# Attention stage: all value products of a unit in one step, the transposes one step later, their split two steps later

## The chip, the cores and the metric

The kernel runs on one core of a Trainium2 chip. The metric is device time in microseconds, the median of three runs. One further execution was recorded by the hardware profiler; its rows are what this text reads.

## What is computed

Two residual layers over 2,048 latent and 256 context tokens of width 1,024. The first is a state-space mixer, the second is grouped-query attention. The change touches the second layer's softmax attention alone:

```
grp = 16 // 4                        # 16 query heads, 4 key/value heads, head size 64
def block(qi):                       # 128 queries
    s = einsum('bqkgd,bskd->bkgqs', qi, k).astype(f32) * 64 ** -0.5    # against 2304 keys
    p = softmax(s, axis=-1)
    return einsum('bkgqs,bskd->bqkgd', p, v)
```

The output of attention is gated, multiplied by the output weights, added to the residual and normalized.

## The kernel before

All of attention is `odd_attention` (from line 1905). A **unit** is one query head with 128 queries against all 2,304 keys, so there are 16 query tiles x 16 heads = 256 units. A unit goes through these steps, each a small function:

- `s_step(u, b)`, for b = 0, 1, 2: four float32 matmuls on TensorE (PE) give the scores of 768 keys in PSUM tile `s` (two buffers). A VectorE (DVE) instruction copies them to `st` (`st0`, `st1`, `st2`, two buffers each) and folds the running maximum into `mx` (L2002). After b = 2 a small DVE instruction makes the exponent's bias of it (L2006).
- `exp_step(u, b)`: ScalarE (ACT) takes the exponential in place (L2010). It needs the bias of L2006.
- `n_step(u, b)` and `d_step(u, b)`, b = 0, 1: GpSimd (POOL) splits the first six (b = 0) or four (b = 1) chunks of 128 keys into a high and a low float16 part (L2017, L2018), and a transposing DMA on SP's queue turns them into `T` (L2022).
- `t_step(u)`: PE transposes the other eight chunks into PSUM tile `tp` (one buffer, L2029).
- `split_step(u)`: ACT copies `tp` to float16 `hi` (L2034). `lower_step(u)`: DVE subtracts, `lo = tp - hi` (L2039). `hi` and `lo` have two buffers.
- `pv_step(u, g)`: products with the values, accumulated in PSUM tile `pv` (one buffer), two for each chunk, one with the high part (129 columns, L2058) and one with the low part (65 columns, L2060). Group g = 0 uses the six chunks of the first DMA (12 products), g = 1 the four of the second (8 products), g = 2 the eight of `hi` and `lo` (16 products). In group 2 the first product takes `hi` and the second takes `lo`.
- `pv_end(u)`: ACT copies the result out (L2073); every fourth unit adds a DVE reciprocal and three small POOL instructions.

The order on every engine is the program order, written by hand: a loop makes one **round** of three steps for each u. In round u the scores are those of unit u + 2, the exponentials those of unit u + 1, the transposes those of unit u, the value products those of unit u - 1. The functions are called in the order shown in the diff below; each call appends to the queues of its engines.

At the end of a step, entries of `todo` follow. `finish` spreads the output projection of a query tile (16 units) over the next rounds: transposes of the result `pt` at step 2 of two rounds, then 16 times three matmuls into `po` (L2116 to L2118), 14 of them at step 2 of consecutive rounds and two at step 1 of two of these rounds, then the normalization, of which `end` (ACT L2127, DVE L2128) stands at step 1 of two rounds. In the first 17 rounds `out_weights` also splits the output weights, at the start of step 2 (ACT L1449, DVE L35 `wl`).

Of the kernel before, what the change touches and what calls it, by code (L numbers as in the profile page):

```python
# [1904 lines left out]
def odd_attention(E, out):  # L1905
    nc, I, S, tc = E.nc, E.I, E.S, E.tc
    v, gp = nc.vector, nc.gpsimd
    with ExitStack() as ctx:
# [38 lines left out]
        def values(i):  # L1947

            cs = slice(3 * i, 3 * i + 3)
            x = RAWV[:, cs].rearrange("p c (k d) -> p (c k) d", d=HD)  # L1950
            vv = V2[:, cs].rearrange("p c k e -> p (c k) e")
            nc.scalar.activation(out=vv[:, :, 0:64], in_=x, func=AF.Copy, scale=E.vscale[:, 0:1])
            if i in VPOOL:
                gp.tensor_scalar(out=x, in0=x, scalar1=E.vscale[:, 0:1], scalar2=0.0, op0=ALU.mult, op1=ALU.add)
                gp.tensor_tensor(out=vv[:, :, 65:129], in0=x, in1=vv[:, :, 0:64], op=ALU.subtract)
            else:
                v.scalar_tensor_tensor(out=vv[:, :, 65:129], in0=x, scalar=E.vscale[:, 0:1], in1=vv[:, :, 0:64],
                                       op0=ALU.mult, op1=ALU.subtract)
# [3 lines left out]
        def out_weights(u, b):  # L1962

            n = u - 1
            k, half = divmod(n, 2)
            if b == 0 and half == 1 and 0 <= k + 1 < KC:
                OW[k + 1] = sp.tile([P, DM], F32, tag=("oh", "ol")[k % 2], name="wr", bufs=1)
                nc.sync.dma_start(out=OW[k + 1], in_=I["od_wo"][:, k + 1])
            if b == 0 and n == 0:
                for w in ("wh", "wl"):  # L1970
                    W[w] = (wp if w == "wh" else vp).tile([P, KC, DM], F32R, tag=w, name=w)
            if b == 2 and 0 < n <= 2 * KC:
                kk, h = divmod(n - 1, 2)
                cs = slice(h * 512, h * 512 + 512)
                split_raw(nc, v, W["wh"][:, kk, cs], W["wl"][:, kk, cs], OW[kk][:, cs])
            if b == 2 and 0 <= n < 2 * KC:
                cs = slice(half * 512, half * 512 + 512)
                gp.tensor_tensor(out=OW[k][:, cs], in0=OW[k][:, cs], in1=gate[:, cs], op=ALU.mult)
# [5 lines left out]
        def unit(u):  # L1984
            return u // 16, (u // 4) % 4, u % 4

        def s_step(u, b):

            qt, kv, hh = unit(u)
            if b == 0:  # L1990
                if hh == 0 and u // 4 + 1 < 64:
                    load_q(u // 4 + 1)
                UN[u] = dict(mx=kp.tile([P, 8], F32, tag="mx", name="mx", bufs=4), st=[None] * NTH)
            U, Q = UN[u], QB[u // 4]
            st = U["st"][b] = pp.tile([P, TH], F32, tag=f"st{b}", name="st", bufs=2)
            mx = U["mx"]
            ps = sps.tile([P, 1024], F32, tag="s", name="s", bufs=2)
            for c0, n in ((0, 512), (512, TH - 512)):
                for i in range(2):
                    nc.tensor.matmul(ps[:, c0:c0 + n], Q[:, hh % 2, i, hh // 2], KS[kv][:, b * TH + c0:b * TH + c0 + n],  # L2000
                                     start=(i == 0), stop=(i == 1))
            v.tensor_tensor_reduce(out=st, in0=ps[:, :TH], in1=zero.to_broadcast([P, TH]), scale=1.0,  # L2002
                                   scalar=NEG if b == 0 else mx[:, b - 1:b], op0=ALU.add, op1=ALU.max,
                                   accum_out=mx[:, b:b + 1])
            if b == NTH - 1:
                v.tensor_scalar(out=mx[:, 6:7], in0=mx[:, b:b + 1], scalar1=-1.0, scalar2=LOGP, op0=ALU.mult, op1=ALU.add)  # L2006

        def exp_step(u, b):
            st = UN[u]["st"][b]
            nc.scalar.activation(out=st, in_=st, func=AF.Exp, bias=UN[u]["mx"][:, 6:7])  # L2010

        def n_step(u, b):

            n = DCH[b] * P
            nat = UN[u]["nat", b] = pp.tile([P, 2, n], F16, tag=f"nat{b}", name="nat", bufs=2)
            p = UN[u]["st"][b][:, :n]
            gp.tensor_scalar(out=nat[:, 0], in0=p, scalar1=1.0, scalar2=0.0, op0=ALU.mult, op1=ALU.add)  # L2017
            gp.tensor_tensor(out=nat[:, 1], in0=p, in1=nat[:, 0], op=ALU.subtract)  # L2018
# [12 lines left out]
        def split_step(u):  # L2031
            hi, lo = [pp.tile([P, TCH, P], F16, tag=n, name=n, bufs=2) for n in ("hi", "lo")]
            pt = UN[u]["pt"]
            nc.scalar.activation(out=hi, in_=pt, func=AF.Copy)  # L2034
            UN[u]["hl"] = hi, lo
# [5 lines left out]
        def pv_step(u, g):  # L2041

            qt, kv, hh = unit(u)
            if g == 0:
                UN[u]["pv"] = sps.tile([P, 130], F32, tag="pv", name="pv", bufs=1)
            pv = UN[u]["pv"]
            c0, n = ((0, DCH[0]), (DCH[0], DCH[1]), (DCH[0] + DCH[1], TCH))[g]
            for k in range(n):
                c = c0 + k
                if g < 2:  # L2050
                    hi, lo = [UN[u]["T", g][:, i * n + k, :] for i in range(2)]
                else:
                    hi, lo = [t[:, k] for t in UN[u]["hl"]]
                first = g == 0 and k == 0
                end = g == 2 and k == n - 1
                for w in (0, 1) if first else (1, 0) if k == n - 1 else (0, 1):
                    if w == 0:
                        nc.tensor.matmul(pv[:, 0:129], hi, V2[:, c, kv, 0:129], start=first, stop=end)  # L2058
                    else:
                        nc.tensor.matmul(pv[:, 0:65], lo, V2[:, c, kv, 0:65], start=False, stop=False)  # L2060

        def pv_end(u):
            qt, kv, hh = unit(u)
            pv = UN[u]["pv"]
            if u % 16 == 3:
                QT[qt] = sp.tile([P, DM], F32, tag="o", name="o", bufs=1)
            if u % 16 == 0:
                SG[qt] = sp.tile([P, DM], F32, tag="sg", name="sg", bufs=1)
                nc.sync.dma_start(out=SG[qt], in_=S["sg"][qt * P:(qt + 1) * P, :])
            if hh == 0:  # L2070
                QR[kv % 2] = sp.tile([P, 4, 130], F32, tag="r", name="r")
            R = QR[kv % 2]
            nc.scalar.activation(out=R[:, hh, 0:129], in_=pv[:, 0:129], func=AF.Copy)  # L2073
            if hh == 3:
                oc = QT[qt][:, kv * 256:(kv + 1) * 256].rearrange("p (h d) -> p h d", d=HD)
                rs = sp.tile([P, 4, 1], F32, tag="rs", name="rs")
                v.reciprocal(rs, R[:, :, 64:65])
                of = QT[qt][:, kv * 256:(kv + 1) * 256]
                sgk = SG[qt][:, kv * 256:(kv + 1) * 256]
                small.extend([  # L2080
                    lambda: gp.tensor_tensor(out=oc, in0=R[:, :, 0:64], in1=R[:, :, 65:129], op=ALU.add),
                    lambda: gp.tensor_tensor(out=oc, in0=oc, in1=rs.to_broadcast([P, 4, HD]), op=ALU.mult),
                    lambda: gp.tensor_tensor(out=of, in0=of, in1=sgk, op=ALU.mult)])
            del UN[u]
            if u % 16 == 15:
                finish(qt, u + 1)
# [64 lines left out]
        for i in range(-2 * NTH, (NU + 2) * NTH):  # L2151
            u, b = divmod(i, NTH)
            if 0 <= i + VSTEP < NS // 3:
                values(i + VSTEP)
            out_weights(u, b)
            live = lambda w: 0 <= w < NU
            if live(u + 2):
                s_step(u + 2, b)
            if b == 1 and live(u):
                split_step(u)  # L2160
            if b == 2 and live(u - 1):
                pv_end(u - 1)
            if live(u + 1):
                exp_step(u + 1, b)
                if b < NTH - 1:
                    n_step(u + 1, b)
            if b == 0 and live(u):
                t_step(u)
            if live(u - 1):
                for g in ((0,), (1, 2), ())[b]:  # L2170
                    pv_step(u - 1, g)
            if live(u + 1) and b < NTH - 1:
                d_step(u + 1, b)
            if b == 1 and live(u):
                lower_step(u)
            if small:
                small.pop(0)()
            for f in todo.pop((u, b), []):
                f()
# [16 lines left out]
def tile_hybrid(ctx, tc, I, out, phases=None, preload=None, dumps=None):  # L2196
# [60 lines left out]
    if on("F"):  # L2257
        odd_attention(E, out)
# [78 lines left out]
```

## Time and profile before

| | |
|---|---|
| time, median of 3 runs | 3898.3 us (3897.76 to 3899.44) |
| the profiled execution | 3896.1 us, span of its instructions 3894.3 us |
| mean granted TensorE clock | 0.983 |
| PE matmul busy | 3692.1 us, 95% of the span |
| DVE busy | 2684.5 us, 69% |
| ACT busy | 1860.5 us, 48% |
| POOL busy | 2192.1 us, 56% |
| attention | about 2430 us to the end |

Busy time is what an engine spends in instructions; the span is from the first to the last instruction. Overlapping matmuls make PE's busy time say little of its reserve: start-to-start times of consecutive groups say more. A DVE or ACT instruction may start a little before the end of the one ahead of it on the same engine.

### The profile page before, as it was taken

To read this page: it belongs to the slowest core of one execution; us is meant where nothing else is said; L and a number is where in the kernel's file an instruction comes from. 1 tells how busy PE (TensorE), PEld (TensorE's weight loads), DVE (VectorE), ACT (ScalarE), POOL (GpSimd) and SP (SyncE) were. 2 spreads that over 40 slices of the span, in tenths; PEclk is the share of its full clock that TensorE was granted. 3 is DMA by queue.
4 is the path that set the end of the run, shared out by engine and by line. 5 is a ranking of instruction groups with operands and counts; after the bars stand their busy time and mean duration, and the time that the engine had idled before them with its cause. 6 is when DMAs were issued, how large, how long until landed. Compare 5 with 4: busy or idle time off the path is not lost. (4 is left out here: it accounts for less than half of the span.)

```text
span 3894.3 us, 72153 instructions
## 1 busy us (share of the span) xinstructions
PE 3692.1 (95%) x27102; PEld 3133.9 (80%) x27102; DVE 2684.5 (69%) x5008; ACT 1860.5 (48%) x3227; POOL 2192.1 (56%) x2120
## 2 busy tenths in 40 slices
PE   7999999977888999999999999799999999999998
PEld 4888886536887888788778887689999999999997
DVE  5367666887786888611354544778888888888885
ACT  4422223424335656311232222667777777777775
POOL 2111113662334999422333323888888888888886
PEclk9999999999999999999999999999999999999999
DMA  7522323335666776534332223998899999999996
GB/s 264 181 61 60 95 78 108 112 116 137 215 228 237 240 240 232 197 115 135 121 119 87 82 91 119 201 153 163 159 169 159 168 166 161 165 158 163 161 166 120
DMA packets 998589, 594.48 MB, mean 153 GB/s; under 512 B 711848, under 2 KB 908248, under 8 KB 996192
## 3 DMA queue, kind: packets, MB, share of 16 engines
q1 hardware_dynamic: 984112, 563.35, 59.7%
q10 hardware_dynamic: 14128, 26.51, 1.9%
q8 instruction: 214, 3.51, 0.4%
q14 instruction: 135, 1.11, 0.1%
HBM read 296.63 MB, written 125.32 MB: 108 GB/s over the span
## 5 line engine op out<-in xcount | busy, mean ns | idle before, releaser
L2010 ACT ACTIVATE st<-st,mx 128x768 f32<-128x768 f32 x768 | 714.3, 930 | 350.2 <-DVE mx L2006 246.0
L2018 POOL TENSOR_TENSOR nat<-st,nat 128x768 f16<-128x768 f32 (+1 forms) x512 | 732.7, 1431 | 42.7
L2000 PE MATMUL s<-KS,q 128*128 128x512 f32 (+1 forms) x3072 | 707.4, 353 | 17.0 <-DVE mx L2002 16.7
L2002 DVE CUSTOM_DVE_ANT_0 st<-s,zero,mx 128x768 f32<-128x768 f32 x512 | 518.9, 1013 | 241.3 <-POOL nat L2017 98.7
L2000 PEld LDWEIGHTS s<-KS,q 128*128 128x128 f32 x3072 | 538.6, 189 | 112.9 <-DVE mx L2002 23.3
L2017 POOL TENSOR_SCALAR nat<-st 128x768 f16<-128x768 f32 (+1 forms) x512 | 378.7, 740 | 128.0 <-ACT st L2010 125.4
L2058 PE MATMUL pv<-V,T 128*128 128x129 f16 x2560 | 310.1, 222 | 14.1 <-DMA T<-nat 14.1
L2039 DVE TENSOR_TENSOR lo<-tp,hi 128x1024 f16<-128x1024 f32 x256 | 312.3, 1220 | 4.6 <-ACT hi L2034 4.6
L41 PE MATMUL mmps<-ah,wh 128*128 128x512 f32 (+1 forms) x800 | 304.6, 381 | 3.8 <-DVE ah L214 3.8
L42 PE MATMUL mmps<-al,wh 128*128 128x512 f32 (+1 forms) x800 | 298.9, 374 | 0.1
L43 PE MATMUL mmps<-ah,wl 128*128 128x512 f32 (+1 forms) x800 | 298.7, 373 | 0.0
L2029 PE MATMUL tp<-ident,st 128*128 128x128 f32 x2048 | 274.7, 275 | 9.9 <-ACT st L2010 5.6
L41 PE MATMUL mm<-w,ah 128*128 128x512 f32 x656 | 263.5, 402 | 1.6 <-ACT ah L1679 1.6
L42 PE MATMUL mm<-w,ah 128*128 128x512 f32 x656 | 256.7, 391 | 2.3 <-DVE w L35 2.3
L2034 ACT ACTIVATE hi<-tp 128x1024 f16<-128x1024 f32 x256 | 257.4, 1006 | 2.7 <-PE tp L2029 1.0
L43 PE MATMUL mm<-w,al 128*128 128x512 f32 x656 | 257.1, 392 | 0.0
L2058 PEld LDWEIGHTS <-T 128*128 128x128 f16 x2560 | 233.6, 97 | 27.2 <-DMA T<-nat 16.2
L2002 DVE CUSTOM_DVE_ANT_0 st<-s,zero 128x768 f32<-128x768 f32 x256 | 243.6, 952 | 13.2 <-PE s L2000 7.3
L2060 PE MATMUL pv<-V,T 128*128 128x65 f16 x2560 | 249.1, 193 | 0.0
L277 DVE SCALAR_TENSOR_TENSOR acc<-raw,convw,acc 128x512 f32<-128x512 f32 (+1 forms) x320 | 223.4, 698 | 35.8 <-POOL raw L270 11.9
L2029 PEld LDWEIGHTS tp<-ident,st 128*128 128x128 f32 x2048 | 229.0, 141 | 22.7 <-ACT st L2010 12.8
L2058 PE MATMUL pv<-V,hi 128*128 128x129 f16 x2048 | 220.3, 220 | 0.0
(431 smaller groups left out, 9006.5 us busy)
## 6 DMA issues: line engine op xcount, KB each, us to landing
ac<-acs SPq DMA_DIRECT2D x72, 512.0 KB
q<-q SPq DMA_DIRECT2D x128, 256.0 KB
x<-xn SPq DMA_DIRECT2D x35, 512.0 KB
h<-h SPq DMA_DIRECT2D x34, 512.0 KB
x<-in_x_dram SPq DMA_DIRECT2D x32, 512.0 KB
adaw<-in_ada_w_dram SPq DMA_DIRECT2D x32, 512.0 KB
a<-aT SPq DMA_DIRECT2D x32, 512.0 KB
wr<-in_ev_w_dram SPq DMA_DIRECT2D x38, 256.0 KB
```

Of the source, the lines that this page charges most:

```text
L41: nc.tensor.matmul(ps, ah(k), bh(k), start=first and k == 0, stop=False)
L42: nc.tensor.matmul(ps, ah(k), bl(k), start=False, stop=False)
L43: nc.tensor.matmul(ps, al(k), bh(k), start=False, stop=last and k == n - 1)
L2000: nc.tensor.matmul(ps[:, c0:c0 + n], Q[:, hh % 2, i, hh // 2], KS[kv][:, b * TH + c0:b * TH + c0 + n], start=(i == 0), stop=(i == 1))
L2002: v.tensor_tensor_reduce(out=st, in0=ps[:, :TH], in1=zero.to_broadcast([P, TH]), scale=1.0, scalar=NEG if b == 0 else mx[:, b - 1:b], op0= ...
L2010: nc.scalar.activation(out=st, in_=st, func=AF.Exp, bias=UN[u]["mx"][:, 6:7])
L2017: gp.tensor_scalar(out=nat[:, 0], in0=p, scalar1=1.0, scalar2=0.0, op0=ALU.mult, op1=ALU.add)
L2018: gp.tensor_tensor(out=nat[:, 1], in0=p, in1=nat[:, 0], op=ALU.subtract)
L2029: nc.tensor.transpose(pt[:, j], UN[u]["st"][b][:, k * P:(k + 1) * P], E.ident)
L2034: nc.scalar.activation(out=hi, in_=pt, func=AF.Copy)
L2039: v.tensor_tensor(out=lo, in0=UN[u]["pt"], in1=hi, op=ALU.subtract)
L2058: nc.tensor.matmul(pv[:, 0:129], hi, V2[:, c, kv, 0:129], start=first, stop=end)
```

## The change

Only the order of the calls within a round, the order of the three product groups, and with it the product that closes the accumulation:

```
-                end = g == 2 and k == n - 1
+                end = g == 1 and k == n - 1
...
             if live(u + 2):
                 s_step(u + 2, b)
-            if b == 1 and live(u):
+            if b == 2 and live(u):
                 split_step(u)
-            if b == 2 and live(u - 1):
+            if b == 1 and live(u - 1):
                 pv_end(u - 1)
             if live(u + 1):
                 exp_step(u + 1, b)
                 if b < NTH - 1:
                     n_step(u + 1, b)
-            if b == 0 and live(u):
+            if b == 0 and live(u - 1):
+                for g in (0, 2, 1):
+                    pv_step(u - 1, g)
+            if b == 1 and live(u):
                 t_step(u)
-            if live(u - 1):
-                for g in ((0,), (1, 2), ())[b]:
-                    pv_step(u - 1, g)
             if live(u + 1) and b < NTH - 1:
                 d_step(u + 1, b)
-            if b == 1 and live(u):
+            if b == 2 and live(u):
                 lower_step(u)
```

Of the engines' queues in a round, with the step's number behind each entry:

```
       before                                             after
PE     s0, T, g0 | s1, g1, g2 | s2                        s0, g0, g2, g1 | s1, T | s2
ACT    exp0 | split, exp1 | pv_end, exp2                  exp0 | pv_end, exp1 | split, exp2
DVE    r0 | r1, lower | r2, bias                          r0 | r1 | r2, bias, lower
```

Here r0 to r2 are the DVE copies of the three score tiles (L2002), and the bias is L2006.

## Rows read from the trace of the kernel before

**Rows 1.** Windows: length, busy PE, PEld, DVE, ACT, POOL, clock, DMA share.
```profile
2470.00:2500.00 30.00, 25.74 (x261) 22.36 (x259) 24.31 (x41) 17.95 (x26) 26.48 (x25) 0.91 1.15 221
2500.00:2530.00 30.00, 25.74 (x278) 21.73 (x278) 25.04 (x47) 20.62 (x30) 29.25 (x28) 1.00 0.78 156
...
2636.40:3778.00 1141.60, 1135.90 (x12381) 1033.81 (x12380) 937.24 (x1795) 823.68 (x1118) 997.31 (x1015) 1.00 0.92 163
```

**Rows 2.** Waits, 2647.7 to 3789: engine, line, releaser, total, times, longest.
```profile
PE s L2000 <- DVE mx L2002: 5.7, 13, 0.5
```

**Rows 3.** Timeline of PE, first transposes of units 0, 32 and 112.
```profile
2434.98 1.91 PE L2029 MATMUL tp<-ident,st 128*128 128x128 f32 x8
...
2636.47 1.04 PE L2029 MATMUL tp<-ident,st 128*128 128x128 f32 x8
...
3075.52 1.04 PE L2029 MATMUL tp<-ident,st 128*128 128x128 f32 x8
```

**Rows 4.** Timeline of PE, one round: start, length, instruction.
```profile
3048.07 1.04 PE L2029 MATMUL tp<-ident,st 128*128 128x128 f32 x8
3048.94 0.22 PE L2058 MATMUL pv<-V,T 128*128 128x129 f16 x1
...
3049.43 0.95 PE L2000 MATMUL s<-KS,q 128*128 128x512 f32 x4
3050.22 0.23 PE L2058 MATMUL pv<-V,T 128*128 128x129 f16 x1
...
3050.64 0.19 PE L2060 MATMUL pv<-V,lo 128*128 128x65 f16 x1
...
3051.25 0.94 PE L2000 MATMUL s<-KS,q 128*128 128x512 f32 x4
...
3052.72 0.86 PE L2000 MATMUL s<-KS,q 128*128 128x512 f32 x4
3053.42 1.04 PE L2029 MATMUL tp<-ident,st 128*128 128x128 f32 x8
```

**Rows 5.** Timeline of DVE over the same round.
```profile
3050.63 1.02 DVE L2002 CUSTOM_DVE_ANT_0 st<-s,zero,mx 128x768 f32<-128x768 f32 x1 [1.13 <-POOL nat L2017]
...
3051.57 1.22 DVE L2039 TENSOR_TENSOR lo<-tp,hi 128x1024 f16<-128x1024 f32 x1
3052.70 1.01 DVE L2002 CUSTOM_DVE_ANT_0 st<-s,zero,mx 128x768 f32<-128x768 f32 x1
...
3053.88 0.96 DVE L2002 CUSTOM_DVE_ANT_0 st<-s,zero 128x768 f32<-128x768 f32 x1
```

**Rows 6.** Timeline of ACT over the same round.
```profile
3051.65 0.93 ACT L2010 ACTIVATE st<-st,mx 128x768 f32<-128x768 f32 x1
...
3054.87 1.00 ACT L2034 ACTIVATE hi<-tp 128x1024 f16<-128x1024 f32 x1
```

**Rows 7.** Timeline: PE transposes followed by scores, and a score group that waited for DVE.
```profile
3002.22 0.60 PE L2101 MATMUL pt<-ident,o 128*128 128x128 f32 x4
...
3002.58 0.95 PE L2000 MATMUL s<-KS,q 128*128 128x512 f32 x4
...
3005.23 0.08 DVE L2002 DVE_READ_ACCUMULATOR2_ANT mx<- 128x1 f32 x1
...
3005.36 0.96 PE L2000 MATMUL s<-KS,q 128*128 128x512 f32 x4 [0.44 <-DVE mx L2002]
```

**Rows 8.** Timeline: a score copy that DVE, free, began on PE's signal.
```profile
3082.24 0.94 PE L2000 MATMUL s<-KS,q 128*128 128x512 f32 x4
...
3083.31 1.02 DVE L2002 CUSTOM_DVE_ANT_0 st<-s,zero,mx 128x768 f32<-128x768 f32 x1 [0.41 <-PE s L2000]
```

**Rows 9.** Groups of instructions, 2700 to 3664 (L2128) and 2440 to 2560 (L35).
```profile
L2128 DVE TENSOR_TENSOR h<-h,fg 128x512 f32<-128x512 f32 x22 | 29.0, 1318 | 0.0
...
L35 DVE TENSOR_TENSOR wl<-wr,wh 128x512 fp32r<-128x512 f32 x16 | 15.5, 969 | 1.4 <-ACT wh L1449 1.3
```

**Rows 10.** Waits, 2440 to 2560.
```profile
PE pv L2058 <- DMA T<-nat: 11.5, 5, 6.4
```

## The prediction

> **What bounds the kernel now.** I read the windows by stage first, then the waits, then the timeline of one round, engine by engine. The windows show that from 2636.4 us on PE is busy 1135.90 of 1141.60 us at a granted clock of 1.00, while DVE is busy 937 and ACT 824 [rows 1]. The waits put all of the 5.7 us that are left to one releaser, DVE's score copies [rows 2]; no wait of PE for a DMA or for `lo` is among them. So the attention stage runs at the sum of PE's start-to-start times. 80 units take 3075.52 - 2636.47 = 439.05 us [rows 3], so a block of 16 takes 87.81 and one unit 5.49 us, and a plain round takes 3053.42 - 3048.07 = 5.35 us [rows 4].
>
> A round on PE, by starts [rows 4]: transposes 0.87, first products 0.49 (12), second scores 0.79, other products 1.03 (24; the first `lo` product starts 0.42 into them, behind eight of the DMA's and one of `hi`), third scores with a piece of the output projection 1.47 (0.79 and 0.68, if these scores take what the second do), first scores 0.70. The sum is 5.35.
>
> What covers DVE now: `lower` ends at 3051.57 + 1.22 = 3052.79 [rows 5], and its first reader is the second product of group 2 of the *next* round, at 3050.64 + 5.35 = 3055.99. It is done 3.20 us before it is needed. DVE is idle 18% of this stretch [rows 1], and none of its instructions sets the pace.
>
> **The change part by part.** No instruction is added or removed; no DMA is added, and the transposing DMAs keep their place in the steps. There are three effects.
>
> *PE's own time.* In the new order a round is scores 0.70, 36 products 0.49 + 1.03 = 1.52, scores 0.79, transposes, scores and projection 1.47. The transposes are now followed by scores, not by products. Four transposes ahead of scores take 3002.58 - 3002.22 = 0.36 us [rows 7]; eight ahead of products take 0.87, 0.109 each. So eight ahead of scores lie between 2 x 0.36 = 0.72 and 0.87; I take 0.36 + 4 x 0.109 = 0.80. The sum is 5.28, a gain of 0.07 us for a plain round.
>
> *The new wait.* `lower` now stands behind the third score copy and the bias on DVE, and its reader is nearer: only the third scores, the projection piece, the next first scores, 12 products and one `hi` product lie between. From the start of the third scores, PE comes to the first `lo` product after 1.47 + 0.70 + 0.49 + 0.05 (one `hi` product, 0.42 / 9) = 2.71 us [rows 4]. DVE from the same start:
>
> - The copy of the third scores begins. With DVE free it began 3083.31 - 3082.24 = 1.07 us after the scores did [rows 8], and 3050.63 - 3049.43 = 1.20 us in the plain round [rows 4, 5]. I take 1.10, since this copy waits for fewer engines than the one of the plain round.
> - From the start of that copy to the start of what follows the bias: 3053.88 - 3052.70 = 1.18 us [rows 5].
> - `lower` itself: 1.22 us [rows 5].
> - DVE's end to PE's start: 3005.36 - (3005.23 + 0.08) = 0.05 us [rows 7].
>
> That is 3.55 us. PE stands 3.55 - 2.71 = 0.84 us in every round, and behind the waiting product its whole queue stands: the rest of the products, the second scores, the transposes, the third scores. These start the next `lower`, so the wait closes a loop: 3.55 + the 23 products from there on 0.98 (0.61 for the 15 of group 2, from 3050.64 to 3051.25, and 0.37 for the eight of group 1) [rows 4] + scores 0.79 + transposes 0.80 = 6.12 us. The new pace is this loop, not PE's sum. Rounds with no projection piece gain nothing by that, since the piece lies in the wait.
>
> Could `split` be later than DVE? It starts after the transposes, whose eight matmuls last 1.04 us [rows 4], so 0.24 us after the third scores begin, and ends 1.00 later [rows 6] at about 1.4; `lower` starts at 2.28. The exponential ahead of it on ACT, which follows `pv_end`, starts 3051.65 - 3051.25 = 0.40 us after the scores that follow the products and lasts 0.93 [rows 4, 6], so it ends at 1.33, while the transposes end at 0.79 + 1.04 = 1.83. So 0.9 us are left there. With that cover gone each 0.1 us would cost 0.1 us a round.
>
> *What is moved.* `pv_end` one step earlier frees `pv` earlier, which nobody waits for. Group 0 comes 0.87 us earlier in a round, since the transposes no longer stand before it, and group 1 about 1.0 us earlier (at 0.70 + 0.49 + 0.66 and not at 0.70 + 0.87 + 0.49 + 0.79). But PE waited for no DMA in the steady stretch [rows 2], and a round gets 0.77 us longer, between one and two rounds of which lie between issue and use. I cost this at nothing. If it weren't covered, PE would show a wait for `T` as it does in the first rounds [rows 10].
>
> **The sum.** In a block of 16 rounds, two have a second projection piece, which now stands after the transposes, inside the loop: 2 x 0.68 = 1.4. Two have `end` at step 1: DVE's L2128 then comes between the second and the third copy. It waits for ACT: the exponential ends 1.33 after the second scores began, L2127 on 512 columns is estimated from the exponential's 768 at 0.93 x 2/3 = 0.62, so it is free at 1.16 after the transposes began; it holds DVE for 1.32 [rows 9], so with a release of 0.1 the third copy starts at about 2.6 and not at 0.80 + 1.10 = 1.90: 2 x 0.7 = 1.4. A block takes 16 x 6.12 + 2.8 = 100.7 us instead of 87.81: +12.9. From unit 32 to the end there are 14 blocks: +181.
>
> The first 32 rounds take 2636.47 - 2434.98 = 201.5 us [rows 3] and are held by DMAs (11.5 us of PE's waits for `T` [rows 10]) and by the splitting of the weights. There DVE's L35, 0.97 us 16 times [rows 9], comes between the second and third copy: the second copy ends at 1.20 + 1.02 - 0.79 = 1.43 after the transposes began, L35 at 2.4, 0.5 later than 1.90. So 16 rounds at 6.6 and 16 at 6.15 are 204; with none or all of the DMA waits added it is +3 to +14. I take +7.
>
> In all +188: 3896.1 + 188 = 4084 for an execution like the profiled one, which lies 2.2 us under the median; so 4086 us. The forecast's own range: the loop with the copy at 1.07 to 1.20, transposes at 0.72 to 0.87, release at 0.05 to 0.15 is 6.01 to 6.39 us, so -25 and +60 over 224 rounds, and first rounds of 0 to +14: 4055 to 4155.
>
> **The rivals.**
>
> *Faster: PE's sum stays the bound.* This needs `lo` within 2.71 us of the start of the third scores, 0.84 us sooner than the rows give; it would be so if `lower` ran ahead of the third copy on DVE. For it: DVE is idle 18% of the stretch [rows 1]. Against: the queue is in program order, and in the trace the order of calls is kept (copy, `lower`, copy) [rows 5]. Its price: 0.07 us in 256 rounds, 18 us, and PE's waits of 5.7 us gone [rows 2]: 3898 - 24 = 3874 us.
>
> *Much slower: the copy of the second scores waits for the transposes.* `st1` has two buffers, so the scores of unit u + 2 overwrite those of unit u, whose last two chunks the transposes of unit u still read, now after the second scores. If that copy waits for the second transpose only, it begins 2 x 0.11 + 0.17 (by which the group's 1.04 exceeds its 0.87) + 0.13 (from PE's end to DVE's start [rows 8]) = 0.52 us after the transposes began, against 1.20 - 0.79 = 0.41 without, and ends before the third copy may start at 1.90: no cost. If it waits for all eight, it begins at 1.04 + 0.13 = 1.17, and the third copy 1.2 later (a copy's 1.02 and an estimated 0.2 to read its maximum). The loop is then 1.17 + 1.2 + 2.45 + 0.98 + 0.79 = 6.59. L2128 now costs its whole 1.4 twice, and the two extra pieces some 0.5: 16 x 6.59 + 3.3 = 108.7 a block, +20.9, 14 times 293, and with the first rounds about +305: 4205 us. The trace has no such case: its copies follow long after the transposes. The first reading is likelier, since only chunks 10 and 11 are `st1`'s.
>
> [...]
>
> **How the numbers follow.** Forecast 0.70, second copy waiting for all transposes 0.12, clock 0.06, faster 0.10, and 0.02 for a wait that happens to cancel. The range from 4040 to 4210 takes in the forecast's own range and the two slower cases, and leaves out the faster one and a tail. A change of under 0.2% is what a measurement here can't tell from none. Faster 0.10, same 0.02, slower 0.88.
>
> **What would show it.** In the profile after: PE waits for DVE's `lo` at L2060 about 0.8 us in a plain round, some 190 us in all, where no such row stands now; transposes of consecutive plain units 6.1 us apart; PE busy about 86% with the clock at 1.00; `lower` directly behind the bias. If PE waits instead for `s` or `tp`, or if the second copy starts over 1 us after the transposes, the second rival holds. The prediction is wrong if `lower` comes out ahead of the third copy, or if `split` ends after the bias.

## The result and the profile after

The changed kernel takes 4072.52 us (median of four runs, 4071.61 to 4076.47) against 3898.03 before: 1.0454 times as long, 95% interval 1.044 to 1.0468. That is 174.5 us more; 188 were forecast. The profiled execution, 4076.47 us, is the slowest of the four; its span is 4074.6 us, 180.3 more than the one before.

The waits come first, from the first transposes of unit 32 to 3949.5 us (engine, line, releaser, total, times, longest).

```profile
DVE st L2002 <- PE tp L2029: 268.5, 206, 1.5
...
PE pv L2060 <- DVE lo L2039: 137.0, 208, 1.7
```

Where PE was held 5.7 us in all [rows 2], it now waits 137.0 us for `lo`, 208 times, at the first `lo` product (L2060). No other releaser holds PE there. DVE in turn waits for PE: the two engines hold each other, as in a loop. The windows of two stretches agree (length, busy PE, PEld, DVE, ACT, POOL, clock, DMA):

```profile
2660.40:3949.50 1289.10, 1152.14 (x12378) 1024.63 (x12377) 939.73 (x1794) 845.88 (x1119) 994.78 (x1015) 1.00 0.76 144
...
2500.00:2530.00 30.00, 20.47 (x244) 18.29 (x245) 24.03 (x40) 18.41 (x25) 26.16 (x24) 1.00 0.78 152
```

PE is busy 1152.14 of 1289.10 us, 89%, and the granted clock is 1.00; so it is in the second window, from 2500 us on, where PE is busy 20.47 of 30 us. From 2530 to 2560 us it was 0.89, with PE busy 22.30 of 30 us, where the kernel before had 1.00 with 25.21. Compare the steady window of before [rows 1].

One round on PE and DVE, from the timeline after:

```profile
3101.63 1.04 PE L2029 MATMUL tp<-ident,st 128*128 128x128 f32 x8
3102.42 0.96 PE L2000 MATMUL s<-KS,q 128*128 128x512 f32 x4
...
3105.14 0.22 PE L2058 MATMUL pv<-V,hi 128*128 128x129 f16 x1
3105.91 0.20 PE L2060 MATMUL pv<-V,lo 128*128 128x65 f16 x1 [0.56 <-DVE lo L2039]
...
3106.88 0.95 PE L2000 MATMUL s<-KS,q 128*128 128x512 f32 x4
3107.66 1.04 PE L2029 MATMUL tp<-ident,st 128*128 128x128 f32 x8
3108.46 0.94 PE L2000 MATMUL s<-KS,q 128*128 128x512 f32 x4
...
3102.14 1.02 DVE L2002 CUSTOM_DVE_ANT_0 st<-s,zero,mx 128x768 f32<-128x768 f32 x1 [1.45 <-PE tp L2029]
...
3103.51 1.02 DVE L2002 CUSTOM_DVE_ANT_0 st<-s,zero,mx 128x768 f32<-128x768 f32 x1 [0.34 <-PE s L2000]
...
3104.64 1.22 DVE L2039 TENSOR_TENSOR lo<-tp,hi 128x1024 f16<-128x1024 f32 x1
```

The loop can be walked: third scores 3102.42, their copy 3103.51, `lower` 3104.64 to 3105.86, first `lo` product 3105.91, second scores 3106.88, transposes 3107.66, the next third scores 3108.46. That is 6.04 us, and the only gaps in it are hand-overs from one engine to the other and the bias ahead of `lower`.

The first transposes of units 0, 32 and 112 show where in the stage the time lies:

```profile
2440.64 1.91 PE L2029 MATMUL tp<-ident,st 128*128 128x128 f32 x8
...
2660.38 1.03 PE L2029 MATMUL tp<-ident,st 128*128 128x128 f32 x8
...
3156.42 1.03 PE L2029 MATMUL tp<-ident,st 128*128 128x128 f32 x8
```

Five blocks of 16 rounds take 3156.42 - 2660.38 = 496.04 us, 99.2 each, where they took 87.8 [rows 3]. The first 32 rounds take 219.7 us, where they took 201.5.

### The profile page after: what moved, and what is told of

It is laid out like the page before. It is cut to its first block, busy times and chain, and to the rows that moved or that the text cites. A ratio compares the mean times of both kernels' runs of the same rounds, so it can differ in the third digit from the quotient of the medians.

```text
span 4074.6 us, 71839 instructions
## 1 busy us (share of the span) xinstructions
PE 3713.6 (91%) x27102; PEld 3131.6 (77%) x27102; DVE 2696.7 (66%) x5008; ACT 1886.7 (46%) x3227; POOL 2190.0 (54%) x2120
## 5 line engine op out<-in xcount | busy, mean ns | idle before, releaser
L2002 DVE CUSTOM_DVE_ANT_0 st<-s,zero,mx 128x768 f32<-128x768 f32 x512 | 520.7, 1017 | 424.5 <-PE tp L2029 330.1
L2018 POOL TENSOR_TENSOR nat<-st,nat 128x768 f16<-128x768 f32 (+1 forms) x512 | 728.9, 1424 | 42.6
L2060 PE MATMUL pv<-V,lo 128*128 128x65 f16 x2048 | 194.6, 194 | 186.7 <-DVE lo L2039 186.7
L2060 PEld LDWEIGHTS <-lo 128*128 128x128 f16 x2048 | 163.6, 98 | 230.7 <-DVE lo L2039 230.7
L2058 PE MATMUL pv<-V,hi 128*128 128x129 f16 x2048 | 255.4, 220 | 0.0
L2060 PE MATMUL pv<-V,T 128*128 128x65 f16 x2560 | 249.0, 193 | 0.0
```

## The experiments

The theory is the loop: third scores, their copy, `lower`, products, second scores, transposes. The rivals are that the grouping of the products, the transposes' new place, DVE's load as such, or late DMAs cost the time. Medians and ratios are those of each run against runs of the kernel before on the same chip; a plain round is the distance of two consecutive transposes in a round without extra work.

**1. Move the reader back: groups in the order 0, 1, 2.**

```
-                for g in (0, 2, 1):
+                for g in (0, 1, 2):
...
-                end = g == 1 and k == n - 1
+                end = g == 2 and k == n - 1
```

> The changed kernel with the product groups in the order 0, 1, 2, so that the eight products of group 1 (0.37 us) come ahead of those with lo. Theory (a loop through lower): between the first lo product and the next second scores lie 15 products and not 23, so a round gets 0.37 us shorter, 240 to 256 times: -89 to -95 us, about 3980 us. Rival (the grouping of all products, or the transposes' new place, costs PE time of its own): no change, 4072 us.

Measured: 3964.20 us (ratio 1.0167, 1.015 to 1.0184), 108 less than the changed kernel; a plain round 3108.92 - 3103.24 = 5.68 us, 0.36 shorter.

```profile
3103.24 1.03 PE L2029 MATMUL tp<-ident,st 128*128 128x128 f32 x8
3108.92 1.03 PE L2029 MATMUL tp<-ident,st 128*128 128x128 f32 x8
```

The order of two groups alone gives back most of the loss, by the number of products left between `lo` and the second scores. The 108 us are more than the 89 to 95 expected. By the transposes' starts, the excess is mostly in the two rounds of each 16 that have L2128, which fall from 6.47 and 7.13 us to 5.87 and 5.88. The same matmuls run, still all in step 0, so their grouping isn't what costs most.

**2. Move `lower` ahead of the third copy on DVE.**

```
+            if b == 2 and live(u):
+                split_step(u)
+                lower_step(u)
             if live(u + 2):
                 s_step(u + 2, b)
-            if b == 2 and live(u):
-                split_step(u)
...
-            if b == 2 and live(u):
-                lower_step(u)
```

> The changed kernel with split and lower called at the start of step 2, so that lower stands ahead of the third score copy on VectorE; nothing else moves. Theory: lower ends about 2.6 to 2.8 us after the third scores begin and not 3.4, PE comes there at 2.71, the wait all but goes, and PE's own sum of 5.28 to 5.45 us sets the round: 3865 to 3915 us. Rival (the second copy's wait for the transposes, or the grouping, costs the time): a round stays above 5.9 us, 4040 us or more.

Measured: 3940.33 us (ratio 1.0109, 1.0094 to 1.0124). The number was missed by 25 us, on the rival's side of the forecast but far from the rival. The timeline of the transposes and of ACT shows both halves:

```profile
3093.58 1.03 PE L2029 MATMUL tp<-ident,st 128*128 128x128 f32 x8
3098.92 1.03 PE L2029 MATMUL tp<-ident,st 128*128 128x128 f32 x8
3105.29 1.04 PE L2029 MATMUL tp<-ident,st 128*128 128x128 f32 x8
3111.79 1.04 PE L2029 MATMUL tp<-ident,st 128*128 128x128 f32 x8
3118.23 1.03 PE L2029 MATMUL tp<-ident,st 128*128 128x128 f32 x8
...
3100.17 1.05 ACT L50 ACTIVATE oh<-h 128x1024 fp32r<-128x1024 f32 x1
...
3101.21 1.01 ACT L2034 ACTIVATE hi<-tp 128x1024 f16<-128x1024 f32 x1
...
3103.53 0.20 PE L2060 MATMUL pv<-V,lo 128*128 128x65 f16 x1 [1.02 <-DVE lo L2039]
```

A plain round takes 5.34 us, as worked out: the loop is gone. But three rounds in 16 now take 6.4 to 6.5. In the first of them ACT's L50 (the normalization's sum of squares, 1.05 us, at step 1) stands ahead of `split`, and PE waits 1.02 us for `lo`. With `lower` ahead, `split` has become the last to arrive, and what stood ahead of it free of charge is charged.

**3 and 4. Lengthen `lower`, after and before.**

```
+            v.tensor_tensor(out=lo[:, 0:2], in0=UN[u]["pt"][:, 0:2], in1=hi[:, 0:2], op=ALU.subtract)
             v.tensor_tensor(out=lo, in0=UN[u]["pt"], in1=hi, op=ALU.subtract)
```

> The changed kernel with a second subtraction on VectorE ahead of lower, over two of its eight chunks (128 x 256), estimated from lower's 1.22 us at 0.3 to 0.4 us. Theory: lower is on the loop, so every round gets longer by all of that: +75 to +100 us, about 4160 us. Rival (VectorE isn't on the path, PE waits by its order): within 10 us of 4072.

> The same second subtraction in the kernel before. Theory: lower has 3.2 us to spare there, so only the four or so rounds in 16 in which VectorE is late for other reasons lengthen: 0 to +15 us, 3898 to 3913 us. Rival (VectorE's load as such sets the pace in either order): +75 to +100 us.

Measured: 4196.57 us after (ratio 1.0762, 1.0746 to 1.0778), 124 more than the changed kernel; 3903.74 before (1.0021, 1.0011 to 1.003), 7 more. The added instruction's group, and two transposes of the changed kernel with it:

```profile
L2039 DVE TENSOR_TENSOR lo<-tp,hi 128x256 f16<-128x256 f32 x144 | 59.8, 415 | 0.0
```
```profile
3099.68 1.04 PE L2029 MATMUL tp<-ident,st 128*128 128x128 f32 x8
3106.18 1.04 PE L2029 MATMUL tp<-ident,st 128*128 128x128 f32 x8
```

It lasts 0.415 us, more than estimated, so the loss is above the 75 to 100 us expected. A plain round grows by 6.50 - 6.04 = 0.46: all of it is on the path. In the old order the same work, 256 times, costs 7 us in all. So DVE's load isn't what sets the pace.

**5 and 6. Keep DVE's order and let PE come later: low parts last.** The groups run in the order 0, 1, 2, and group 2 as

```
+            if g == 2:
+                order = [(k, 0) for k in range(n - 1)] + [(k, 1) for k in range(n)] + [(n - 1, 0)]
```

where 0 is a product with `hi` and 1 one with `lo`. The second of the two kernels also moves the normalization:

```
-            at = sorted(at) + [(w + 17, 1), (w + 18, 1), (w + 19, 1), (w + 20, 1)]
+            at = sorted(at) + [(w + 17, 2), (w + 18, 2), (w + 19, 2), (w + 20, 2)]
```

> The changed kernel with the groups in the order 0, 1, 2, and in group 2 seven products with hi first, then all eight with lo, then the last with hi. VectorE's order stays as changed. Theory: PE comes to the first lo product 0.37 + 7 x 0.057 = 0.77 us later, at 3.48 us after the third scores begin, about when lower is done (3.4 to 3.5): the wait is gone without any engine getting faster, a plain round takes PE's sum, 5.28 to 5.4 us, and the time is 3880 to 3925 us. Rival (the grouping or the transposes' new place cost PE time themselves): a plain round stays above 5.6 us, over 3960 us.

> The same, with the normalization of a query tile (four entries of finish) at step 2 in place of step 1, behind the bias and lower on VectorE and behind the third exponential on ScalarE. Theory: the rounds in which L2128 or L50 delays the third copy or split lose their extra 0.4 to 1.1 us, about 1.5 us in 16 rounds: 15 to 25 us less than the run before it, 3860 to 3905 us. Rival (these rounds are long for another reason): no difference.

Measured: 3906.87 us (1.0027, 1.0017 to 1.0036) and 3896.87 us (1.0001, 0.9992 to 1.0011). In the first, a plain round takes

```profile
3104.75 1.03 PE L2029 MATMUL tp<-ident,st 128*128 128x128 f32 x8
3110.09 1.04 PE L2029 MATMUL tp<-ident,st 128*128 128x128 f32 x8
```

5.34 us, and PE's waits from 2660 to 3760 us are these (`lo`'s product stands at L2063 here, the product with `T` at L2061):

```profile
PE pv L2063 <- DVE lo L2039: 13.0, 22, 1.1
PE pv L2061 <- DMA T<-nat: 7.4, 8, 2.2
```

No engine works less than in the changed kernel and DVE's queue is the same; only the order of the products has changed, so that the one that waits comes 0.77 us later on PE (as worked out in the expectation), and 166 us are back. That is the strongest of the runs for the loop. All products are still in one step and the transposes still in their new place, 11 us over the kernel before on the same chip (3906.87 - 3895.97), so neither can be what costs the 174.5. The second kernel gained 10 us of the 15 to 25 expected.

**7 and 8. The normalization at step 2**, by the same edit, in the kernel of experiment 2 and in the changed kernel.

> The kernel with lower ahead of the third copy (3940 us), with the normalization at step 2 in place of step 1. In that run plain rounds took 5.33 us as worked out, but three rounds in 16 took 6.3 to 6.5. Theory: ScalarE's L50 and L2127 stand ahead of split there, and VectorE's L2128 behind it ahead of the third copy; moved, these rounds go to about 5.4: 3.0 us in 16 rounds, 42 us less, 3885 to 3910 us. Rival (waits for the DMA's T, which also show there, make these rounds long): within 10 us of 3940.

> The changed kernel with only the normalization moved to step 2. Theory: the two rounds of 6.47 and 7.13 us in 16 go to 6.03, which measures what the prediction counted as 2 x 0.7 us for L2128: 1.5 us in 16 rounds, 21 us less than the changed kernel, 4045 to 4058 us. Rival (the long rounds are not L2128's): 4072 us.

Measured: 3915.16 us (1.0045, 1.0029 to 1.0062), 25 less than without the move, not 42; and 4047.18 us (1.0387, 1.0371 to 1.0402), 25 less than the changed kernel, against 21 expected. The second fits the size of the term for L2128, though the edit moves the rest of the normalization with it. The first is between theory and rival. From 2660 to 3760 us PE no longer waits for `lo`, but its waits for the DMA have grown; experiment 2 first, then this kernel:

```profile
PE pv L2058 <- DMA T<-nat: 8.2, 18, 1.1
...
PE pv L2058 <- DMA T<-nat: 23.3, 34, 2.1
```

The growth of 15 us is about the 17 that are missing. A reason that fits, but was not tried by itself: `lower` ahead of the third copy delays the bias, with it the exponentials and the DMA's input, and the products are earlier than in the old order.

**9. The kernel before with the normalization at step 2.**

> The kernel before with only the normalization of a query tile moved from step 1 to step 2. Theory (a late third copy is what costs rounds their time): the rounds of 6.08 and 5.83 us in each 16 go to about 5.4, 1.1 us in 16 rounds, 14 times: 15 us less, 3875 to 3888 us. Rival (those rounds are long for the normalization's other work): no change, 3896 us.

Measured: 3888.31 us (0.9973, 0.9962 to 0.9984), just above what was expected: 8 of the 15 us came. It is the only kernel of this study faster than both, by 0.3%. From 2680 to 3700 us PE's waits for DVE's copies [rows 2] are gone, and 1.3 us of waits for `T` have come.

**10. Split and `lower` at step 2, nothing else.**

```
-            if b == 1 and live(u):
+            if b == 2 and live(u):
                 split_step(u)
...
-            if b == 1 and live(u):
+            if b == 2 and live(u):
                 lower_step(u)
```

> The kernel before with split and lower moved to step 2, behind the third copy, and nothing else: transposes and products stay where they were. lower's first product is then still over 1 us away, but the transposes of the next unit, one step on, write the single tile tp that lower reads. Theory (what counts is who waits for lower): they stand until lower is done, 3.45 us after the third scores begin where PE comes at 1.47 + 0.70 = 2.17; a loop of 3.5 + 0.87 + 0.49 + 0.79 + 1.03 = 6.65 us, about 4200 us (4170 to 4240). Rival (only the products' wait for lo matters, or only the grouping of the products): within 20 us of 3896.

Measured: 4249.49 us (1.0898, 1.0881 to 1.0914), 9 us above the expected range. Two transposes of the timeline:

```profile
3102.49 1.09 PE L2029 MATMUL tp<-ident,st 128*128 128x128 f32 x8 [1.16 <-DVE lo L2039]
3109.19 1.09 PE L2029 MATMUL tp<-ident,st 128*128 128x128 f32 x8 [1.14 <-DVE lo L2039]
```

The round is 6.70 us (6.65 forecast), and it is the transposes that wait for `lower`, to write `tp` over. As the theory had it, who waits for `lower` is what counts: here another wait closes a loop through it. Of the change, this half alone costs more than the whole.

**11 and 12. All products in step 0, nothing else.** From the changed kernel:

```
-            if b == 2 and live(u):
+            if b == 1 and live(u):
                 split_step(u)
...
-            if b == 1 and live(u):
+            if b == 0 and live(u):
                 t_step(u)
...
-            if b == 2 and live(u):
+            if b == 1 and live(u):
                 lower_step(u)
```

The second of these kernels also has the normalization at step 2.

> The changed kernel with transposes back at step 0 (behind the products), split and lower back at step 1, so that of the change only the grouping of all products in step 0 and the earlier copy of pv are left. Theory: lower is done long before the products, PE's own sum sets the round, 5.30 to 5.35 us in a plain one, and the time is 3880 to 3905 us. Rival (36 products in one go cost by themselves, through PE's time, the clock or T coming late): 3950 us or more.

> The run before it with the normalization at step 2. Theory: one us less in 16 rounds, 12 to 18 us less, 3865 to 3890 us; the grouping then is worth 0.05 us a round at most against the kernel before with the same move, 0 to 13 us. Rival: T is late now and then, as in the run with the low parts last, and the grouping loses that gain: 5 to 20 us over the kernel before with the same move.

Measured: 3930.98 us (1.0083, 1.007 to 1.0097) and 3929.62 us (1.0081, 1.0069 to 1.0094). Both numbers were missed: the grouping alone isn't free but costs 35 us against the kernel before on the same chip (3930.98 - 3896.21), less than the rival's 50 or more. Rows of PE's transposes, PE's weight loads and DVE's copies of the first, and then a row of its waits from 2680 to 3700 us:

```profile
3062.64 1.04 PE L2029 MATMUL tp<-ident,st 128*128 128x128 f32 x8
...
3068.08 1.04 PE L2029 MATMUL tp<-ident,st 128*128 128x128 f32 x8
...
3065.70 0.30 PEld L2000 LDWEIGHTS s<-KS,q 128*128 128x128 f32 x2 [0.37 <-DVE mx L2002]
...
3064.62 1.02 DVE L2002 CUSTOM_DVE_ANT_0 st<-s,zero,mx 128x768 f32<-128x768 f32 x1 [1.23 <-POOL nat L2017]
3065.57 0.08 DVE L2002 DVE_READ_ACCUMULATOR2_ANT mx<- 128x1 f32 x1
```
```profile
PE pv L2058 <- DMA T<-nat: 12.2, 19, 1.4
```

A plain round takes 5.44 us and not 5.30, 0.09 more than before [rows 4]; over 256 rounds that would be an estimated 23 us. With the products gone from step 1, second scores, third scores, projection and first scores stand in a row on PE. The `s` tile has two buffers, so the first scores write over the second, and stand until the second copy has ended (3065.65; they start at 3065.70). The products between scores were a cover for DVE's copies. This wait is what the theory left out. In the changed kernel the transposes stand between second and third scores, and no such wait shows there. The other part is what the rival named, `T` coming late: the 12.2 us of the last row have no counterpart in the steady stretch of the kernel before [rows 2]. Moving the normalization gave back 1.4 us here, so the second kernel is 41 us over that of experiment 9 (3929.62 - 3888.31), more than theory or rival said; why the move gave so little stays open.

## Why the prediction was right

**The bound and the new wait.** Right. The wait was named with its place (the first `lo` product, behind the third copy and the bias), and the profile after shows it there and, from unit 32 on, nowhere else. "Some 190 us in all" were forecast; in the page of the profile the group has 186.7 us of idle time ahead of it:

```profile
L2060 PE MATMUL pv<-V,lo 128*128 128x65 f16 x2048 | 194.6, 194 | 186.7 <-DVE lo L2039 186.7
```

**The loop, term by term.** Copy 1.10 forecast, 1.09 measured; copy to `lower` 1.18, 1.13; `lower` 1.22, 1.22; release 0.05, 0.05; products 0.98, 0.97; scores 0.79, 0.78; transposes 0.80, 0.80. The sum is 6.04 and not 6.12; the one term clearly off is the way from the copy to `lower`, which was read from another instruction behind the bias.

**PE's own time.** Forecast 5.28; with no wait left it is 5.34 in experiments 2 and 5, as good as the 5.35 of before [rows 4]. The 0.07 us a round that the new order was to save on PE isn't there to be had, and so neither were the 18 us of the faster rival; in the changed kernel it is hidden by the wait in any case. The wait of a plain round, forecast at 0.84 us, is 0.72: the first `lo` product starts 0.77 us after the `hi` product ahead of it (3105.91 - 3105.14), where 0.05 was counted. The shorter loop (0.08) and PE's longer sum (0.06) about make up the difference.

**The extra work in the loop.** L2128 was counted as 1.4 us in a block, 0.7 in each of two rounds. By the transposes' starts the two are 0.43 and 1.09 us longer than 6.04, so 1.5 in all; moving the normalization (experiment 8) gave back 25 us, of which 21 were expected from the rounds. A block took 99.2 us and not 100.7, mainly for the 0.08 us in each round's loop: 14 blocks x 11.4 = 160 us and not 181.

**The first rounds: mis-sized.** They cost 18.2 us and not 7. The term that was mis-sized is the length of L35 there, taken as 0.97 us between the second and the third copy. The tile's view, before and after (times in ns: least, median, most; after, two of the 16 fall behind the window):

```profile
L35 DVE TENSOR_TENSOR wl<-wr,wh x16: 679/692/2179, 2453.8 to 2556.2; 128x512 fp32r<-128x512 f32 x16
```
```profile
L35 DVE TENSOR_TENSOR wl<-wr,wh x14: 665/1621/2142, 2457.0 to 2556.1; 128x512 fp32r<-128x512 f32 x14
```

And one of them after, with the POOL instruction beside it and PE's wait:

```profile
2517.94 1.17 POOL L2018 TENSOR_TENSOR nat<-st,nat 128x512 f16<-128x512 f32 x1
...
2517.99 1.67 DVE L35 TENSOR_TENSOR wl<-wr,wh 128x512 fp32r<-128x512 f32 x1
2519.58 1.00 DVE L2002 CUSTOM_DVE_ANT_0 st<-s,zero,mx 128x768 f32<-128x768 f32 x1
...
2521.97 0.20 PE L2060 MATMUL pv<-V,lo 128*128 128x65 f16 x1 [2.28 <-DVE lo L2039]
```

The mean of 0.97 hid very different lengths: in the old order nine of the 16 took 0.68 or 0.69 us and the others 0.92 to 2.18; in the new order nine take 1.58 to 1.68. In the row shown L35 starts just after a POOL instruction that it overlaps, and ends 0.55 us after that one's end at 2519.11; the shortest L35 after took 0.67 in all, so most of the 1.67 us is waiting, by the author's estimate. The kernel before has both orders of start:

```profile
2504.61 1.65 POOL L2018 TENSOR_TENSOR nat<-st,nat 128x768 f16<-128x768 f32 x1
...
2517.91 2.18 POOL L2018 TENSOR_TENSOR nat<-st,nat 128x768 f16<-128x768 f32 x1
...
2504.63 2.18 DVE L35 TENSOR_TENSOR wl<-wr,wh 128x512 fp32r<-128x512 f32 x1
...
2517.89 0.68 DVE L35 TENSOR_TENSOR wl<-wr,wh 128x512 fp32r<-128x512 f32 x1
```

The one that starts second, by 0.02 us, is the one that takes longer: L35 2.18 us and not 0.68, L2018 2.18 and not 1.65. `lower` shows nothing of the kind: at 2477.51 in the kernel before it lay wholly beside an L2018 and took 1.22 us, and in both traces every one took 1.21 to 1.23. No experiment moved L35, so that POOL's instruction held it is read from the trace and not tried. Over all 16 its mean is 1.42 us, which makes 7 of the 11 us that were missed; the rest is open. The remaining difference of the spans, 2440.64 - 2434.98 = 5.7 us, lies before the first transposes. It is scatter: in experiment 8, whose calls up to there are those of the changed kernel, they start at 2434.53.

**The sum.** The blocks were forecast 21 us too long and the first rounds 11 us too short. That these partly cancel, so that the forecast of 4086 us is only 13 us off, is in part luck.

**The rivals.** The second copy does wait for the transposes, as the second rival asked, but it starts 3102.14 - 3101.63 = 0.51 us after they began, which fits a wait for the second of the eight (0.52 was worked out) and not for all (1.17), and is no cost. This rival's sum is about 2 us off (3898 + 305 is 4203); nothing hangs on it. The granted clock was 1.00 from 2660.40 to 3949.50 us, with PE busy 89%. No run shows what a lower clock costs a round, so the forecast's chance of 0.06 for it, and its part as one of the two slower cases in the range, were the author's estimate. The faster case would have needed `lower` to come earlier; experiment 2 put it there, and even then other waits kept it at 3940 us.

## What to carry to other kernels

When two in-order queues hand work to each other, write down for each hand-over how long before its reader the result is ready, and check after a reordering whether the chain of hand-overs closes within one round: then its length (here 6.04 us), not the busiest engine's sum (PE's 5.34), is the pace. The place of the *reader* is as good a lever as the producer's: moving the waiting product 0.77 us down the queue gave back 166 us at no cost. A mean over instructions of one kind that meet different neighbours (0.97 us from 0.68 to 2.18) isn't a price for a new place.

## What the runs showed of the hardware

After the reciprocal L2077, every fourth round, the third copy began 0.98 us after its scores (3109.44 - 3108.46) and not 1.09, and that round was 0.1 us shorter:

```profile
3109.12 0.18 DVE L2077 RECIPROCAL rs<-r 128x4 f32<-128x4 f32 x1
3109.44 1.02 DVE L2002 CUSTOM_DVE_ANT_0 st<-s,zero,mx 128x768 f32<-128x768 f32 x1
```

In the plain rounds from 2704 to 2960 us it is 0.98 to 1.00 us behind the reciprocal and 1.07 to 1.10 without it. So with a small extra instruction ahead of it, the waiting one started sooner after PE's signal. Why wasn't tried.
